# A recurrent branch's elementwise products and a small memset, moved from GpSimd to VectorE and ScalarE

## The chip, the cores and the metric

The kernel runs on one core of a Trainium2 chip. A core has several engines that each work through their own list of instructions in order and wait for each other by semaphores: TensorE (PE in the profile; its weight loads are listed apart as PEld), VectorE (DVE), ScalarE (ACT), GpSimd (POOL) and SyncE (SP). Transfers between the chip's memory (HBM) and the core's own (SBUF) are issued by an engine and then run on DMA engines; in this kernel SP and POOL issue them. The metric is the device time of one execution in microseconds (us).

## The reference

One layer of a hybrid decoder, in fp32: a prompt of 2048 positions (behind 16 learned meta positions) and 8 sequences that are continued by 8 positions each from a paged cache.

```python
hn = rmsnorm(x, g_mix_pre)
q, k, v, xl, gate = split(hn @ w_in)
attn = attend(q, k, v)          # stick-breaking: weights from sigmoids and a running product
lru, h_last, conv_last = rglru_branch(xl, ...)
mixed = concat([attn, lru * gelu(gate)]) @ w_out
x = x + rmsnorm(mixed, g_mix_post)
u = relu(rmsnorm(x, g_mlp_pre) @ w_up)
x = x + rmsnorm((u * u) @ w_down, g_mlp_post)

# rglru_branch: xc = causal convolution of width 4 over xl
r = sigmoid(xc @ w_gate_a + b_gate_a);  i = sigmoid(xc @ w_gate_x + b_gate_x)
log_a = -8 * softplus(-lru_lambda) * r
a = exp(log_a);  b = sqrt(-expm1(2 * log_a)) * (i * xc)
h[t] = a[t] * h[t-1] + b[t]
```

The change touches the products i * xc and those of gelu(gate), the columns that the convolution carries from one block to the next, and the clearing of one attention operand.

## The kernel before

**Precision.** Matrix products of fp32 are made of three matmuls each: both operands are split in a rounded part (hi) and a remainder (lo), and hi·hi, lo·hi and hi·lo are summed (L181 to L183; L213 to L215 with the operands' roles exchanged). For each piece of weights of 128 x 1024, `w_split` (L151 ff) has ACT write whi (L158) and DVE write wlo = wraw - whi (L159). whi and wlo have two buffers each, so the split of one piece runs while PE works on the piece before.

**Stages.** The prompt goes in four blocks of 512 positions (block 0 also carries the 16 meta and 64 sample positions, 592 columns in all). For each block s: the input projection `inproj`, attention, output projection and MLP. In `inproj` the recurrent branch comes first, in four columns c of 128 channels: a matmul for x_lru, evacuated by ACT into xp (L501) behind three columns carried over from the block before (L499), whose last three columns are kept for the next (L502); the convolution on DVE into xc (L505, L507); a matmul for the gate, evacuated by ACT into g (L521); and GeLU of it as g * sigmoid(g * (G1 * g^2 + G0)), in L524 to L528. `gates` (L443 to L457) makes r and ii by small matmuls (L452) and sigmoids on ACT (L453), and multiplies ii by xc (L454). `recur` (L459 to L486), once for columns 0 and 1 and once for 2 and 3, has tanh, exp and sqrt on ACT, two products on DVE (L469, L470), the recurrence as a scan on DVE (L478), the product with GeLU of the gate (L483), and the store to md in HBM. Keys, values and queries follow.

**The order of the work.** PE's order is written out by hand: generators for attention, the sample's attention and the projections are interleaved by a budget of PE time (`work.tick`, with a rate per stage), and this order is fixed. The other engines' lists are set by a scheduler under the same dependencies.

**The sample's attention** (`sample_attn`, L823 ff) runs in four groups t, interleaved with the projections of blocks 1 and 2. POOL gathers cache pages with indirect DMAs (`page`, L831) into buffers of the tag kv (three of them); two gathers fill one buffer. PE uses the key pages at L854 and the value pages at L883. The transposed weights of a group are copied into a buffer of the tag q (two of them).

**Attention of the prompt** (`attn`). POOL loads for each head h the queries q(h), 512 KB, into the same tag q (L667), and key and value pieces (L671, L672, and L684 to L692 into the tag kv). `chain` makes weights beta from logits: two sigmoids on ACT (L640, L641), a scan on DVE (L645 or L648), a copy of the carry (L651) and a product (L652). `emit_T` transposes the weights on PE (L712) and has them split into wth (ACT, L723) and wtl (DVE, L724); for the key block that holds the 16 meta positions, wth alone is cleared whole (L718) and then filled in two bands of 16 rows (ACT L719, DVE L720). wth has three buffers. `emit_V` multiplies with the values (L734, L736).

**Norms.** The power -0.5 in each rmsnorm is on POOL (L237), as is a product in the MLP's end (L1079).

Of the kernel before, what the change touches and what calls it, by code (L numbers as in the profile page):

```python
# [8 lines left out]
F32 = mybir.dt.float32  # L9
# [4 lines left out]
ALU = mybir.AluOpType  # L14
# [70 lines left out]
def _program(tc, I, O, NSB, NSC):  # L85

    nc = tc.nc
# [343 lines left out]
    def inproj(s, p1, pa, K, ahi, alo, before_k=None):  # L431
# [14 lines left out]
        def gates(c, xc):  # L446
            r = T(p1, [P, W], F32, "r", 2)[:, 0:N]
            ii = T(p1, [P, W], F32, "ii", 2)[:, 0:N]
            for gi, dst, bv in ((1, ii, "bx"), (0, r, "ba")):
                for (a, b) in chunks:  # L450
                    o = psD()
                    nc.tensor.matmul(o[:, 0:b - a], K["gw"][:, gi, c, :], xc[:, a:b], start=True, stop=True)  # L452
                    nc.scalar.activation(dst[:, a:b], o[:, 0:b - a], AF.Sigmoid, bias=K[bv][:, c:c + 1])  # L453
            nc.gpsimd.tensor_tensor(ii, ii, xc[:, 0:N], op=ALU.mult)  # L454
            rs.append(r)
            iis.append(ii)
            work.tick(1.5)  # L457
# [31 lines left out]
        for c in range(4):  # L489
            outs = gemm(hi_, lo_, chunks, before_k=before_k if c == 0 else None)  # L490
            if held is not None:
                gates(*held)
            if c == 2:
                recur((0, 1))
            xp = T(p1, [P, 3 + W], F32, "xp")
            if s == 0:
                nc.gpsimd.memset(xp[:, 0:3], 0.0)
            else:
                nc.gpsimd.tensor_copy(xp[:, 0:3], K["convc"][:, c, :])  # L499
            for (a, b), o in zip(chunks, outs):  # L500
                nc.scalar.copy(xp[:, 3 + a:3 + b], o)  # L501
            nc.gpsimd.tensor_copy(K["convc"][:, c, :], xp[:, NP:NP + 3])  # L502
            cw = K["cw"]
            xc = T(p1, [P, W], F32, "xc", 1)
            nc.vector.tensor_scalar(xc[:, 0:NP], xp[:, 0:NP], cw[:, c, 0:1], K["cb"][:, c:c + 1], op0=ALU.mult, op1=ALU.add)  # L505
            for j in range(1, 4):
                nc.vector.scalar_tensor_tensor(xc[:, 0:NP], xp[:, j:j + NP], cw[:, c, j:j + 1], xc[:, 0:NP],  # L507
                                               op0=ALU.mult, op1=ALU.add)
            if s == 0:
                spad = T(p1, [P, DB, DS + 3], F32, "spad", 2)  # L510
                nc.gpsimd.tensor_copy(spad[:, :, 0:3], K["sconv"][:, c])
                nc.gpsimd.tensor_copy(spad[:, :, 3:3 + DS], xp[:, 3 + NP:3 + N].rearrange("p (b t) -> p b t", b=DB))
                nc.gpsimd.tensor_copy(K["csamp"][:, c], spad[:, :, DS:DS + 3])
                xs = xc[:, NP:N].rearrange("p (b t) -> p b t", b=DB)
                nc.vector.tensor_scalar(xs, spad[:, :, 0:DS], cw[:, c, 0:1], K["cb"][:, c:c + 1], op0=ALU.mult, op1=ALU.add)
                for j in range(1, 4):
                    nc.vector.scalar_tensor_tensor(xs, spad[:, :, j:j + DS], cw[:, c, j:j + 1], xs, op0=ALU.mult, op1=ALU.add)
            outs = gemm(hi_, lo_, chunks)
            g = T(p1, [P, W], F32, "g")
            for (a, b), o in zip(chunks, outs):  # L520
                nc.scalar.copy(g[:, a:b], o)  # L521
            g = g[:, 0:N]
            gt = T(p1, [P, W], F32, "gt", 2)[:, 0:N]
            nc.gpsimd.tensor_tensor(gt, g, g, op=ALU.mult)  # L524
            nc.gpsimd.tensor_scalar(gt, gt, G1, G0, op0=ALU.mult, op1=ALU.add)
            nc.gpsimd.tensor_tensor(gt, gt, g, op=ALU.mult)
            nc.scalar.activation(gt, gt, AF.Sigmoid)
            nc.gpsimd.tensor_tensor(gt, gt, g, op=ALU.mult)  # L528
            gts.append(gt)
            held = (c, xc)  # L530

# [124 lines left out]
    def attn(s, K):  # L656
# [51 lines left out]
        def emit_T(it):  # L708
            t = psT()
            kn, i0 = it["kn"], it["i0"]  # L710
            for (i, w, c0) in it["parts"]:
                nc.tensor.transpose(t[0:kn, i * P:(i + 1) * P], w[:, c0:c0 + kn], ident)  # L712
            cs = slice(i0 * P, 512)
            hi = T(att, [P, SB], F32R, "wth", 3)
            if kn < P:

                lo = None
                nc.gpsimd.memset(hi.bitcast(F32), 0.0)  # L718
                nc.scalar.copy(hi[0:kn, cs], t[0:kn, cs])  # L719
                nc.vector.tensor_tensor(hi[32:32 + kn, cs], t[0:kn, cs], hi[0:kn, cs].bitcast(F32), op=ALU.subtract)  # L720
            else:
                lo = T(att, [P, SB], F32R, "wtl", 3)
                nc.scalar.copy(hi[:, cs], t[:, cs])  # L723
                nc.vector.tensor_tensor(lo[:, cs], t[:, cs], hi[:, cs].bitcast(F32), op=ALU.subtract)  # L724
            live["w"] -= it["frees"]
            it.update(hi=hi, lo=lo, cs=cs, at=step[0] + 4)
            vq.append(it)
            return 0.6 * (4 - i0) / 4
# [565 lines left out]
```

## Time and profile before

| | |
|---|---|
| runs | 2783.65, 2796.56, 2788.62 us; median 2788.62 |
| the profiled execution | 2790.22 us, of which its span, the time that the trace covers, is 2788.3 us |
| mean clock granted to PE | 0.985 of full speed |
| busy: PE, DVE, ACT, POOL | 2688.2, 1814.3, 1451.6, 515.5 us |
| PE idle by the trace | about 100 us |

In the profile, a row such as "L159 DVE TENSOR_TENSOR wlo<-wraw,whi" names the line of the kernel, the engine, the operation and the tiles written and read. Idle time of an engine is put down to what ended it, its releaser; "issue" is time for which no releaser shows. The clock that is granted to PE is given as a share of full speed, and falls to one half in some stretches. The busy time of an engine in a stretch shows whether it could be what others wait for there; which wait ended last shows whether it was.

### The profile page before, as it was taken

To read this page: it belongs to the slowest core of one execution; us is meant where nothing else is said; L and a number is where in the kernel's file an instruction comes from. 1 tells how busy PE (TensorE), PEld (TensorE's weight loads), DVE (VectorE), ACT (ScalarE), POOL (GpSimd) and SP (SyncE) were. 2 spreads that over 40 slices of the span, in tenths; PEclk is the share of its full clock that TensorE was granted. 3 is DMA by queue.
4 is the path that set the end of the run, shared out by engine and by line. 5 is a ranking of instruction groups with operands and counts; after the bars stand their busy time and mean duration, and the time that the engine had idled before them with its cause. 6 is when DMAs were issued, how large, how long until landed. Compare 5 with 4: busy or idle time off the path is not lost.

```text
span 2788.3 us, 36998 instructions
## 1 busy us (share of the span) xinstructions
PE 2688.2 (96%) x13804; PEld 2219.4 (80%) x13804; DVE 1814.3 (65%) x2790; ACT 1451.6 (52%) x2426; POOL 515.5 (18%) x711
## 2 busy tenths in 40 slices
PE   8999988998899999999999999999999999999998
PEld 6886766777688888887788888878888887998996
DVE  5456364686777777788867777798686436433434
ACT  6556364575665655565555555665555234332332
POOL 5336361341211101112110001120000002000002
PEclk9999998999999999999999999999999999999999
DMA  4465855467534433345443333454333334322223
GB/s 161 134 208 189 261 152 171 134 169 221 166 92 128 119 115 106 106 138 154 154 110 115 103 111 103 138 162 143 105 96 104 112 119 144 99 84 77 83 84 113
DMA packets 177316, 368.23 MB, mean 132 GB/s; under 512 B 49153, under 2 KB 79361, under 8 KB 177137
## 3 DMA queue, kind: packets, MB, share of 16 engines
q1 hardware_dynamic: 103792, 287.35, 32.2%
q0 software_dynamic: 73344, 78.52, 11.3%
q8 instruction: 109, 1.79, 0.3%
q14 instruction: 71, 0.57, 0.1%
HBM read 305.51 MB, written 60.04 MB: 131 GB/s over the span
## 4 chain that ended last, share of the span: by engine, by line
PE 80%; DVE 7%; DMA 5%; POOL 3%; issue 3%; ACT 2%; SPq 0%; POOLq 0%; DVEq 0%; ACTq 0%
PE D L181 11%; PE D L183 11%; PE D L182 11%; PE D L213 10%; PE D L214 10%; PE D L215 10%; PE T L712 4%; PE T L702 4%; PE O L734 2%; PE O L736 2%; DVE wlo L159 1%; DMA md<-pb 1%; DVE pb L648 1%; POOL rstd L237 1%; DMA q<-qd 1%
## 5 line engine op out<-in xcount | busy, mean ns | idle before, releaser
L159 DVE TENSOR_TENSOR wlo<-wraw,whi 128x1024 fp32r<-128x1024 f32 x368 | 464.2, 1261 | 496.1 <-ACT whi L158 495.8
L181 PE MATMUL D<-ahi,whi 128*128 128x512 f32 (+3 forms) x1920 | 709.2, 369 | 0.0
L183 PE MATMUL D<-ahi,wlo 128*128 128x512 f32 (+3 forms) x1920 | 686.3, 357 | 2.0 <-DVE wlo L159 2.0
L182 PE MATMUL D<-alo,whi 128*128 128x512 f32 (+3 forms) x1920 | 685.0, 357 | 2.8 <-DVE alo L1017 1.5
L158 ACT CAST whi<-wraw 128x1024 fp32r<-128x1024 f32 x368 | 386.6, 1050 | 485.5 <-PE D L214 282.8
L213 PE MATMUL D<-whi,uh 128*128 128x512 f32 x1024 | 418.1, 408 | 0.0
L183 PEld LDWEIGHTS D<-ahi,wlo 128*128 128x128 f32 x1920 | 364.8, 190 | 53.2 <-DVE wlo L159 2.9
L181 PEld LDWEIGHTS D<-ahi,whi 128*128 128x128 f32 x1920 | 365.2, 190 | 51.9 <-issue 8.7
L214 PE MATMUL D<-whi,ul 128*128 128x512 f32 x1024 | 405.2, 396 | 0.0
L215 PE MATMUL D<-wlo,uh 128*128 128x512 f32 x1024 | 404.3, 395 | 0.0
L182 PEld LDWEIGHTS D<-alo,whi 128*128 128x128 f32 x1920 | 365.7, 190 | 45.5 <-DVE alo L1017 1.7
L640 ACT ACTIVATE keep<-T,nbias 128x512 f32<-128x512 f32 (+6 forms) x352 | 209.7, 596 | 241.7 <-PE T L702 234.6
L648 DVE TENSOR_TENSOR_SCAN pb<-keep,carry 128x513 f32<-128x513 f32 (+1 forms) x228 | 270.3, 1186 | 71.9 <-ACT keep L640 69.9
L724 DVE TENSOR_TENSOR wtl<-T,wth 128x512 fp32r<-128x512 f32 (+1 forms) x320 | 191.0, 603 | 73.7 <-ACT wth L723 72.6
L723 ACT CAST wth<-T 128x512 fp32r<-128x512 f32 (+1 forms) x320 | 166.1, 523 | 127.6 <-PE T L712 122.7
L215 PEld LDWEIGHTS D<-wlo,uh 128*128 128x128 f32 x1024 | 192.7, 188 | 46.7
L213 PEld LDWEIGHTS D<-whi,uh 128*128 128x128 f32 x1024 | 192.9, 188 | 39.9 <-DVE uf L1032 0.4
L214 PEld LDWEIGHTS D<-whi,ul 128*128 128x128 f32 x1024 | 193.3, 189 | 38.6
L652 DVE TENSOR_TENSOR beta<-beta,pb 128x512 f32<-128x512 f32 (+7 forms) x360 | 208.2, 578 | 0.0
L641 ACT ACTIVATE beta<-T,bias 128x512 f32<-128x512 f32 (+6 forms) x352 | 208.2, 591 | 0.0
L712 PE MATMUL T<-ident,beta 128*128 128x128 f32 (+1 forms) x1216 | 193.7, 277 | 14.1 <-ACT beta L641 7.6
L702 PE MATMUL T<-kv,q 128*128 128x512 f32 (+5 forms) x640 | 180.4, 364 | 10.3 <-ACT beta L641 4.4
(235 smaller groups left out, 3600.0 us busy)
## 6 DMA issues: line engine op xcount, KB each, us to landing
wraw<-in_w_up SPq DMA_DIRECT2D x128, 512.0 KB, 3.5
wraw<-in_w_down SPq DMA_DIRECT2D x128, 512.0 KB, 3.5
wraw<-in_w_in SPq DMA_DIRECT2D x64, 512.0 KB, 3.9
q<-qd POOLq DMA_DIRECT2D x32, 512.0 KB, 16.9
wraw<-in_w_out SPq DMA_DIRECT2D x32, 512.0 KB, 3.5
kv<-kd POOLq DMA_DIRECT2D x48, 256.0 KB, 4.1
kv<-vd POOLq DMA_DIRECT2D x48, 256.0 KB, 4.2
y<-in_x_prompt SPq DMA_DIRECT2D x16, 512.0 KB, 5.6
```

The source lines that it names most:

```text
L158: nc.scalar.copy(hi, r)
L159: nc.vector.tensor_tensor(lo, r, hi.bitcast(F32), op=ALU.subtract)
L181: nc.tensor.matmul(o, whi[:, k, :], ahi(k, a, b), start=(k == 0), stop=False)
L182: nc.tensor.matmul(o, whi[:, k, :], alo(k, a, b), start=False, stop=False)
L183: nc.tensor.matmul(o, wlo[:, k, :], ahi(k, a, b), start=False, stop=(k == KC - 1))
L213: nc.tensor.matmul(o, h, whi[:, kk, :], start=st, stop=False)
L214: nc.tensor.matmul(o, l, whi[:, kk, :], start=False, stop=False)
L215: nc.tensor.matmul(o, h, wlo[:, kk, :], start=False, stop=sp)
L640: nc.scalar.activation(keep[:, o:512], S, AF.Sigmoid, bias=nbias, scale=-0.125)
L648: nc.vector.tensor_tensor_scan(pb[:, o:513][:, ::-1], kr, kr, 1.0 if carry is None else carry, op0=ALU.mult, op1=ALU.bypass)
L702: nc.tensor.matmul(o, H["q"][:, e, i * P:(i + 1) * P], kap, start=(e == 0), stop=(e == 1))
L712: nc.tensor.transpose(t[0:kn, i * P:(i + 1) * P], w[:, c0:c0 + kn], ident)
```

## The change

Four edits, all of which take work from POOL's list. L454, ii times xc, goes to DVE. The copies of three columns (L499, L502) go to ACT. GeLU's argument, three steps on POOL (L524 to L526), becomes two steps on DVE, (g * G1) * g and then (that + G0) * g; the last product (L528) goes to DVE too. The memset of wth in `emit_T` (L718) goes to DVE. POOL keeps the loads, the gathers, the norms' powers and a few small steps. From the old L526 on, the changed kernel's line numbers are one less.

```diff
@@ gates
-            nc.gpsimd.tensor_tensor(ii, ii, xc[:, 0:N], op=ALU.mult)
+            nc.vector.tensor_tensor(ii, ii, xc[:, 0:N], op=ALU.mult)
@@ inproj
-                nc.gpsimd.tensor_copy(xp[:, 0:3], K["convc"][:, c, :])
+                nc.scalar.copy(xp[:, 0:3], K["convc"][:, c, :])
             for (a, b), o in zip(chunks, outs):
                 nc.scalar.copy(xp[:, 3 + a:3 + b], o)
-            nc.gpsimd.tensor_copy(K["convc"][:, c, :], xp[:, NP:NP + 3])
+            nc.scalar.copy(K["convc"][:, c, :], xp[:, NP:NP + 3])
...
             gt = T(p1, [P, W], F32, "gt", 2)[:, 0:N]
-            nc.gpsimd.tensor_tensor(gt, g, g, op=ALU.mult)
-            nc.gpsimd.tensor_scalar(gt, gt, G1, G0, op0=ALU.mult, op1=ALU.add)
-            nc.gpsimd.tensor_tensor(gt, gt, g, op=ALU.mult)
+            nc.vector.scalar_tensor_tensor(gt, g, G1, g, op0=ALU.mult, op1=ALU.mult)
+            nc.vector.scalar_tensor_tensor(gt, gt, G0, g, op0=ALU.add, op1=ALU.mult)
             nc.scalar.activation(gt, gt, AF.Sigmoid)
-            nc.gpsimd.tensor_tensor(gt, gt, g, op=ALU.mult)
+            nc.vector.tensor_tensor(gt, gt, g, op=ALU.mult)
@@ emit_T
-                nc.gpsimd.memset(hi.bitcast(F32), 0.0)
+                nc.vector.memset(hi.bitcast(F32), 0.0)
```

PE's list is the same in both kernels. POOL's shrinks from 654 rows to 512, DVE's grows from 2771 to 2867, ACT's from 2301 to 2329. Two places show how the rows now stand.

The first is POOL's list in block 2's input projection, where the sample's attention ends and the attention of block 1 begins: `L831` (`L830`) are gathers of value pages, `L667` (`L666`) the load of q(0), `L684` (`L683`) a load of keys. Before:

```order
L454 TENSOR_TENSOR ii_3649<-ii_3649,xc_3556 128x512
L499 COPY xp_4865<-convc_240 128x3
L524 TENSOR_TENSOR gt_3699<-g_3697 128x512
L525 TENSOR_SCALAR gt_3699<-gt_3699 128x512
L667 DMA q_3925<-qd_78 128x1x1024
L526 TENSOR_TENSOR gt_3699<-gt_3699,g_3697 128x512
L528 TENSOR_TENSOR gt_3699<-gt_3699,g_3697 128x512
L454 TENSOR_TENSOR ii_3765<-ii_3765,xc_3661 128x512
L831 DMA kv_3835<-in_cache_v,ix_199 128x512 x2
L684 DMA kv_3935<-kd 128x400
```

And now:

```order
L830 DMA kv_3745<-in_cache_v,ix_199 128x512 x2
L830 DMA kv_3765<-in_cache_v,ix_199 128x512 x2
L830 DMA kv_3803<-in_cache_v,ix_199 128x512 x2
L666 DMA q_3913<-qd_78 128x1x1024
L830 DMA kv_3823<-in_cache_v,ix_199 128x512 x2
L683 DMA kv_3923<-kd 128x400
```

The load of q(0) stood behind two steps of the GeLU argument and now stands directly behind the group's third pair of gathers; the fourth pair stood behind L454 and now follows the load.

The second is DVE's list in block 3's input projection, at the recurrence of a column (L469 to L483) and the split of the next weights (L159). Before:

```order
L469 SCALAR_TENSOR_TENSOR b_5121<-r_5111,b_5121 128x512
L470 TENSOR_TENSOR b_5121<-b_5121,ii_5112 128x512
L159 TENSOR_TENSOR wlo_5196<-wraw_5153,whi_5195 128x1024
L478 SCALAR_TENSOR_TENSOR ii_5112<-r_5111,hcar_241,b_5121 128x512
L480 COPY hcar_241<-ii_5112 128x1
L483 TENSOR_TENSOR gt_5043<-ii_5112,gt_5043 128x512
```

And now:

```order
L469 SCALAR_TENSOR_TENSOR b_5107<-r_5097,b_5107 128x512
L524 SCALAR_TENSOR_TENSOR gt_5175<-g_5173 128x512
L470 TENSOR_TENSOR b_5107<-b_5107,ii_5098 128x512
L525 SCALAR_TENSOR_TENSOR gt_5175<-gt_5175,g_5173 128x512
L478 SCALAR_TENSOR_TENSOR ii_5098<-r_5097,hcar_241,b_5107 128x512
L159 TENSOR_TENSOR wlo_5181<-wraw_5139,whi_5180 128x1024
L480 COPY hcar_241<-ii_5098 128x1
L483 TENSOR_TENSOR gt_5030<-ii_5098,gt_5030 128x512
L527 TENSOR_TENSOR gt_5175<-gt_5175,g_5173 128x512
```

Two products (L524, L525) and the scan (L478) now stand ahead of the weights' remainder wlo (L159), which stood third; the last product (L527) follows at the end.

## The prediction

> **What bounds the kernel now.** I read the page's engine shares first, then the windows by stage, then what TensorE (PE) waits for, and last the timelines around those waits.
>
> ```profile
> PE 2688.2 (96%) x13804; PEld 2219.4 (80%) x13804; DVE 1814.3 (65%) x2790; ACT 1451.6 (52%) x2426; POOL 515.5 (18%) x711
> ```
>
> PE is busy for 96% of a span of 2788.3 us. Unless the change shortens the matmuls themselves, which it does not, only the other 100 us and the stretches at half clock can be won. By share, GpSimd (POOL) is the engine with the least to do. So I went to the stages in which the moved work stands: the in-projections of the four blocks (26:110, 170:245, 355:430, 500:600) and one stretch of attention. Columns: length in us, then busy time (and instructions) of PE, weight load, DVE, ACT and POOL, the granted clock, the DMA share, GB/s.
>
> ```profile
> 26.00:110.00 84.00, 78.22 (x514) 71.62 (x514) 51.99 (x92) 57.80 (x89) 44.63 (x59) 1.00 0.33 107
> 170.00:245.00 75.00, 75.00 (x457) 55.29 (x456) 53.68 (x68) 52.70 (x80) 41.44 (x39) 1.00 0.51 159
> 355.00:430.00 75.00, 65.32 (x364) 44.28 (x363) 45.66 (x51) 45.34 (x62) 50.30 (x53) 0.91 0.51 143
> 500.00:600.00 100.00, 90.53 (x418) 71.05 (x417) 74.75 (x111) 68.88 (x109) 43.40 (x50) 0.96 0.42 122
> 1400.00:1800.00 400.00, 399.99 (x1918) 329.43 (x1917) 305.88 (x466) 228.27 (x381) 45.18 (x78) 1.00 0.38 112
> ```
>
> Here the picture turns: in block 2's in-projection POOL is busy 50.30 of 75 us, more than DVE or ACT, and PE loses about 10 us and a tenth of its clock. Block 1's has a PE without a gap, and so has attention at 1400:1800. What PE waits for in these places (us in total, times, longest):
>
> ```profile
> PE O L883 <- DMA kv<-in_cache_v,ix: 10.5, 3, 7.7
> PE T L702 <- DMA q<-qd: 6.0, 1, 6.0
> PE D L183 <- DVE wlo L159: 2.0, 1, 2.0
> PE D L452 <- ACT xp L501: 1.4, 2, 0.8
> PE D L452 <- ACT sf L541: 0.6, 1, 0.6
> ```
>
> Together 20.5 us, and behind the larger waits the clock falls to half:
>
> ```profile
> 391.00:394.50 3.50, 3.50 (x10) 2.72 (x9) 2.15 (x3) 3.43 (x6) 2.61 (x3) 0.51 0.76 214
> 415.00:425.00 10.00, 4.94 (x24) 2.83 (x25) 1.71 (x4) 1.52 (x3) 1.74 (x4) 0.50 0.63 137
> 446.00:452.50 6.50, 5.89 (x17) 4.95 (x18) 2.49 (x9) 2.04 (x6) 0.00 (x0) 0.50 0.56 173
> ```
>
> Busy time at half clock is half lost. None of these waits names POOL, yet the DMAs of the first two are issued by POOL, in order, behind its arithmetic. The next views are POOL's and PE's timelines (start, duration, engine, line, in brackets the idle time before and its releaser).
>
> ```profile
> 242.10 1.60 POOL L526 TENSOR_TENSOR gt<-gt,g 128x512 f32<-128x512 f32 x1
> 243.85 1.01 POOL L831 DMA_INDIRECT kv<-in_cache_v,ix  x1
> 380.25 0.95 POOL L831 DMA_INDIRECT kv<-in_cache_v,ix  x1 [0.30 <-issue]
> 401.66 0.91 POOL L667 DMA_DIRECT2D q<-qd  x1
> 406.64 1.75 POOL L454 TENSOR_TENSOR ii<-ii,xc 128x512 f32<-128x512 f32 x1 [0.73 <-ACT ii L453]
> 408.55 1.30 POOL L831 DMA_INDIRECT kv<-in_cache_v,ix  x1 [0.17 <-issue]
> ```
> ```profile
> 238.66 0.64 PE L883 MATMUL O<-kv,q 128*32 128x128 f32 x16
> 247.89 0.43 PE L883 MATMUL O<-kv,q 128*32 128x128 f32 x8 [1.65 <-DMA kv<-in_cache_v,ix]
> 249.50 0.42 PE L883 MATMUL O<-kv,q 128*32 128x128 f32 x8 [1.18 <-DMA kv<-in_cache_v,ix]
> 406.21 0.65 PE L883 MATMUL O<-kv,q 128*32 128x128 f32 x16
> 420.06 0.65 PE L883 MATMUL O<-kv,q 128*32 128x128 f32 x8 [7.69 <-DMA kv<-in_cache_v,ix]
> ```
>
> **The 7.69 us wait** (kv has three buffers). PE's L883 from 406.21 to 406.86 frees the one that the last gathers need. POOL issues them at 408.55, once L454 (ready at 406.64, 1.75 long) is through. And they land late: the answer for the gathers of 362 to 385, and for these two,
>
> ```profile
> DMA to landing us min/median/max: 3.3/3.5/5.1
> DMA to landing us min/median/max: 10.8/11.1/11.5
> ```
>
> The difference of 7.6 us has one visible cause: q(0), issued 6.9 us earlier on the same queue and still under way. From issue to landing such a load takes 16.9 us (median of 32):
>
> ```profile
> q<-qd POOLq DMA_DIRECT2D x32, 512.0 KB, 16.9
> ```
>
> **The change, part by part.** The order of the PE instructions is unchanged.
>
> **(d) q(0) and the last gathers.** In the changed order q(0) stands right behind the third pair of gathers, so it is issued near 381.3 instead of 401.7. With 16.9 us it lands near 398, before the last gathers are issued, at 406.9 (buffer free) instead of 408.55. These then land in 3.3 to 5.1 us for the first and some 1.6 more for the second, near 412, where PE comes to them. Gap 7.69 to near 0.3: -7.4. PE's 4.94 busy us at half clock become 2.5: -2.5. Sum -9.9. Lower bound of this gain, if q(0) still covers the gathers: the earlier issue alone, 1.65.
>
> **(b) the pair at 243.85.** Its buffer was free at 239.30 (238.66 + 0.64) but POOL ran the GeLU argument until 243.70. Without that the pair goes out 4.4 us earlier, more than both waits (1.65 + 1.18): -2.8. Bounds 0 and -2.8.
>
> **(c) wlo at 388.** DVE's row of work ahead of the PE wait (first, two DVE rows; then PE's):
>
> ```profile
> 384.33 2.00 DVE L648 TENSOR_TENSOR_SCAN pb<-keep,carry 128x513 f32<-128x513 f32 x1
> 387.27 1.69 DVE L652 TENSOR_TENSOR beta<-beta,pb 128x512 f32<-128x512 f32 x1
> 390.15 0.50 PE L183 MATMUL D<-ahi,wlo 128*128 128x512 f32 x1 [1.98 <-DVE wlo L159]
> ```
> ```profile
> L648 DVE TENSOR_TENSOR_SCAN pb<-keep,carry 128x513 f32<-128x513 f32 (+1 forms) x228 | 270.3, 1186 | 71.9 <-ACT keep L640 69.9
> L652 DVE TENSOR_TENSOR beta<-beta,pb 128x512 f32<-128x512 f32 x148 | 102.7, 694 | 0.0
> ```
>
> The two ran 0.8 and 1.0 us over their means while POOL was at L524 to L528. Without POOL's arithmetic they should run at the mean; but the new order puts one product of 0.78 us (L524) ahead of this wlo. Net 1.0 of the 1.98 us, and the 3.5 us at 0.51 clock that follow (half of it, 1.7 us, lost) go only if the gap falls below what triggers them. Bounds 0 and -3.7; I take -2.7, nearer the gain since wlo itself also ran under POOL's work.
>
> The Trainium skill, in "TensorE: Matmul & The Clock Gate", Part 1 ("What's actually happening"), says that the clock halves after an idle window of about 3.4 us. By that a gap of 1.98 us would leave the clock alone, and this term would be 1.7 us smaller. The trace has the half clock right behind 1.98 us, so I keep the row.
>
> **(a) block 0.** ACT waits in order for POOL's argument, with the next PSUM evacuation behind it:
>
> ```profile
> 48.61 0.70 ACT L527 ACTIVATE gt<-gt 128x592 f32<-128x592 f32 x1 [3.67 <-POOL gt L526]
> 49.22 0.37 ACT L501 COPY xp<-D 128x272 f32<-128x272 f32 x1
> ```
>
> Two DVE steps in place of three POOL steps, and in the new order L501 stands ahead of L527. PE's waits at L452 for such an evacuation (xp and sf) sum to 2.0 us. I take -2.0, the whole; bounds 0 and -2.0.
>
> **(e) q(1).** The 6.0 us wait and the 5.89 us at half clock (2.9 lost). Its buffer is freed by the last value matmuls of the sample, behind (d), and PE needs it as much later; nothing of POOL's arithmetic stands between. Bounds 0 and -8.9. I take -1.0, the end to which the unchanged order points, with a little for the faster stretch before.
>
> **(f) the new work on DVE.** 64 products (four per column, four columns, four blocks). Nearest rows:
>
> ```profile
> L469 DVE SCALAR_TENSOR_TENSOR b<-r,b 128x512 f32<-128x512 f32 x12 | 9.3, 778 | 7.1 <-ACT b L466 7.0
> L470 DVE TENSOR_TENSOR b<-b,ii 128x512 f32<-128x512 f32 x12 | 9.0, 750 | 0.5
> L526 POOL TENSOR_TENSOR gt<-gt,g 128x512 f32<-128x512 f32 x12 | 19.9, 1661 | 0.9
> L718 POOL MEMSET wth<- 128x512 f32 x32 | 16.8, 525 | 201.5 <-PE O L734 198.4 <-DMA wraw<-in_w_in 2.3 <-issue 0.8
> ```
>
> Half are of the first kind, half of the second: 48 x 0.764 = 36.7 us, and 16 of 592 columns, scaled by width, 14.1: 51 us in all, 12 to 14 per in-projection. DVE goes from 45.66 to about 58 of 75 in block 2, from 53.68 to 66 in block 1, and from 74.75 to 87 of 100 in block 3, the last before any relief by POOL's silence. So the cover holds on average; where it is gone a product ahead of a late wlo costs its 0.76 us, at most 48 times, 37 us. That is the upper bound; 0 is taken, as block 1 has PE gapless beside a DVE that is as busy as block 2's will be. Contention is the other sign: if what L648 and L652 lost at 384 to 389 (1.8 us) is won back in each of the 12 columns of blocks 1 to 3, DVE gains 22.
>
> The 32 memsets (row L718) go to DVE, which has no memset of this size in the trace. Bounds 0 and POOL's 0.525, the one row of the same shape; I take the upper: 17 us. They stand where DVE idles (94 of 400 us in 1400:1800, with PE at 399.99), so 0. On DVE the memset waits in order for a free wth buffer, for which POOL waited 198.4 us in all; queued behind is the next chain's scan, for which ACT's and PE's next transposes wait. With the old times I get 11.5 us of such waiting over 32, all inside existing idle time. If it were not hidden: 17 + 11.5 = 28 us.
>
> The 28 carry copies of 3 columns on ACT: at most 0.37 us each, what L501 takes for 272 columns, so under 10.4 us over four stages of which each leaves ACT over 20 us idle: 0. POOL's rstd powers get an emptier queue; they stand in other stages: 0. Around 745 to 780 DVE's order of the out-projection's work is reshuffled: +-4, taken as 0.
>
> **Sum.** (a) -2.0, (b) -2.8, (c) -2.7, (d) -9.9, (e) -1.0, (f) 0: -18.4. The profiled execution took 2790.22 us, 1.6 over the runs' median of 2788.62. So 2771.8 against its own time, 2770.2 against the median: **2771 us**.
>
> **The rivals.**
>
> **R2: the queue relief is hidden.** The gathers are short of something else than q(0) (a weight load of 512 KB goes out beside them; DMA share 0.63 in 415:425), or q(0) moved forward now covers the third pair instead. Then (d) shrinks to the earlier issue, -1.65, and a change of that size in a 7.69 us gap leaves the half clock. (a), (b), (c) and (e) at half their values, -4.2: 2790.2 - 5.9 = 2784.3. For it: q takes 16.9 us wherever it is issued, and something pays. Against: between 381 and 400 PE needs no gather on short notice. It also covers the case that POOL's queue was not what held the issue.
>
> **R3: DVE takes POOL's place.** DVE is in order. The first product, L524, waits for the store of the old gt, and the last one (L527 in the changed kernel, where lines from 526 on stand one higher up) for ACT's sigmoid, and wlo is queued behind them. Where wlo then comes after PE's need, PE pays what it paid at 388: 1.98 + 1.7 = 3.7. It decides once wlo is late by more than its slack. In blocks 1 to 3 are 12 columns: 44 us, and (c) falls away: 2790.2 - 15.7 + 44.4 = 2818.9. For it: the new order in block 3 does put wlo behind two products, and DVE will be at 87 of 100 there. Against: in block 2 DVE today waits for POOL in the same columns:
>
> ```profile
> DVE xc L505 <- POOL ii L454: 16.2, 10, 2.4
> ```
>
> These 16.2 us of idle time disappear and pay for 21 of the 64 products. By the idle window of 3.4 us (the Trainium skill, "TensorE: Matmul & The Clock Gate", Part 1) this rival would cost 12 x 2.0 = 24 us, without the clock, and end near 2798.
>
> **How the numbers follow.** Forecast 0.55, own range 2761 to 2779 (terms (c), (e) and (f) each +-4). R2 0.33, around 2784. R3 0.12, 2795 to 2820. For 8 in 10 I leave out R3's most and the best ends of (a) and (e): **2757 to 2793**. About 0.5% is what a measurement of this kernel can tell: faster means under 2774.7, slower over 2802.6. Faster: most of the forecast's own cases, 0.50. Slower: R3 where it is full, 0.08. Same: 0.42.
>
> **What would show it.** Right: the wait L883 for in_cache_v gone or under 1 us; q(0) issued near 381; the value gathers near 407 landing in 3 to 5 us; clock 1.00 between 415 and 425; ACT's sigmoid (now L526) with hardly an idle time before it; POOL without a wait between q(0) and the gathers but for the buffer. Wrong: a PE wait for wlo larger than 2 us in all, new stretches at half clock in blocks 1 to 3, a wait of DVE for the gt store with wlo behind it, or wth memsets on DVE with PE's L712 and L734 waits grown beyond their present share. If (d) is there and the time is not, the gain was given back between 430 and 600.

## The result, and the profile after

| | before | changed |
|---|---|---|
| median | 2789.36 us (5 runs) | 2756.25 us (5 runs) |
| lowest to highest | 2783.65 to 2796.56 | 2753.42 to 2759.63 |
| span of the profiled execution | 2788.3 us | 2751.6 us |
| mean clock granted to PE | 0.985 | 0.991 |

The ratio is 0.988, with a 95% interval of 0.986 to 0.990: the change makes the kernel 33 us faster. 2771 was predicted, from 2757 to 2793, so the direction was right, the size was not, and the time lies just below the range. The changed kernel's page has these engine shares:

```profile
PE 2671.6 (97%) x13804; PEld 2207.3 (80%) x13804; DVE 1834.9 (67%) x2886; ACT 1455.6 (53%) x2454; POOL 373.6 (14%) x571
```

POOL lost 142 us of work, DVE got 21 us more: 61 us of products and memsets came (45.1 and 15.5 by their groups), so the rest of its work became 40 us shorter. PE's busy time fell by 17 us though its matmuls are the same, since fewer of them ran at half clock (mean clock 0.985, then 0.991). The same stretches as before (block 0, 2 and 3; each block starts a little earlier now):

```profile
26.00:110.00 84.00, 82.66 (x566) 78.30 (x567) 62.86 (x114) 61.84 (x98) 17.71 (x40) 1.00 0.39 124
355.00:430.00 75.00, 68.10 (x377) 50.47 (x376) 50.79 (x82) 51.00 (x82) 18.30 (x26) 0.95 0.64 187
500.00:600.00 100.00, 99.12 (x463) 78.84 (x461) 81.94 (x148) 78.30 (x133) 14.49 (x28) 1.00 0.57 164
```

The last row surprises: block 3's stretch, in which I had expected nothing, went from 90.53 to 99.12 us of PE in 100 and from clock 0.96 to 1.00. What PE still waits for between 36 and 600 us:

```profile
PE T L701 <- DMA q<-qd: 6.9, 1, 6.9
PE T L711 <- ACT beta L640: 4.6, 1, 4.6
PE T L261 <- DVE wtl L723: 2.7, 1, 2.7
PE T L701 <- DVE alo L264: 1.5, 1, 1.5
PE T L853 <- DMA kv<-in_cache_k,ix: 0.7, 1, 0.7
```

The waits for value gathers, for wlo and at L452 are gone; that for q(1) stayed. POOL's timeline at the load of q(0), and PE's at the last value pages:

```profile
367.03 0.95 POOL L830 DMA_INDIRECT kv<-in_cache_v,ix  x1 [0.30 <-issue]
367.98 0.90 POOL L666 DMA_DIRECT2D q<-qd  x1
392.24 1.00 POOL L830 DMA_INDIRECT kv<-in_cache_v,ix  x1 [23.35 <-PE O L882]
```
```profile
391.50 0.64 PE L882 MATMUL O<-kv,q 128*32 128x128 f32 x16
397.24 0.64 PE L882 MATMUL O<-kv,q 128*32 128x128 f32 x16
399.40 0.43 PE L882 MATMUL O<-kv,q 128*32 128x128 f32 x8
```

q(0) goes out directly behind the third pair, 24 us ahead of the last pair, and the last pair as soon as its buffer is free (391.50 + 0.64 = 392.14). PE finds the pages there.

**Where the time came from.** Both kernels run the same 13804 matmuls in the same order, and so do all the kernels below. So the start of the n-th matmul can be compared between any two traces. The table shows by how much each stretch became longer (+) or shorter (-) than in the profiled execution of the kernel before; the stretches are given in that execution's time. The kernels beside the changed one are those of the experiments.

| stretch, us | changed | gelu | prod | nomem | nocarry | qsp | force | busy16 |
|---|---|---|---|---|---|---|---|---|
| 9 to 36, start | -2.2 | -4.6 | -4.3 | -2.6 | +2.2 | -3.0 | -4.8 | -2.9 |
| 36 to 114, block 0 | -5.6 | -5.6 | -5.6 | -5.6 | -5.1 | 0.0 | -0.8 | -0.7 |
| 244 to 250, gathers | -3.1 | -2.8 | -2.8 | -3.1 | -3.1 | -0.1 | +0.7 | +3.4 |
| 384 to 398, wlo | -3.8 | -3.8 | -3.8 | -3.8 | -3.8 | -1.6 | -1.3 | -3.8 |
| 412 to 428, last gathers | -10.1 | -3.8 | -6.1 | -10.1 | -5.5 | -5.9 | +1.6 | +4.3 |
| 439 to 453, q(1) | 0.0 | -1.9 | +0.3 | +0.6 | -1.5 | -4.2 | -2.1 | +0.2 |
| 579 to 605, block 3 | -6.4 | -6.1 | -6.1 | -6.0 | -6.4 | -0.8 | -4.9 | -6.4 |
| 605 to 678, queries | -0.2 | +4.4 | +6.1 | +5.0 | +1.4 | +2.6 | +3.3 | +2.3 |
| 678 to 693 | -1.9 | +0.4 | -0.3 | -2.2 | -1.0 | -2.7 | 0.0 | -0.5 |
| all else | -3.3 | -1.7 | -0.7 | -3.1 | -4.6 | +1.3 | +5.3 | -2.6 |

The first row is chance: kernels that touch nothing there (memset and carry alone, below) show -4.6 and -4.0. At the start a pair of PE's transposes takes 0.63 us and, from some point on, 0.38; that point came at 29.2 us in the profiled execution of the kernel before and at 23.7 in the changed one's. Rows in which an edit has no cause differ by up to 3 us too (qsp has -2.7 at 678 to 693), and "all else", which is most of the kernel, by up to 5 (force). The rows of the changed kernel from block 0 to 693 sum to -31.1.

### The profile page after: what moved, and what is told of

The parts are those of the page before. It is cut to its first block, busy times and chain, and to the rows that moved or that the text cites. A ratio compares the mean times of both kernels' runs of the same rounds, so it can differ in the third digit from the quotient of the medians.

```text
span 2751.6 us, 36954 instructions
## 1 busy us (share of the span) xinstructions
PE 2671.6 (97%) x13804; PEld 2207.3 (80%) x13804; DVE 1834.9 (67%) x2886; ACT 1455.6 (53%) x2454; POOL 373.6 (14%) x571
## 4 chain that ended last, share of the span: by engine, by line
PE 84%; DVE 7%; DMA 4%; issue 2%; ACT 1%; POOL 1%; SPq 0%; DVEq 0%; POOLq 0%; ACTq 0%
PE D L181 12%; PE D L183 12%; PE D L182 12%; PE D L213 10%; PE D L214 10%; PE D L215 10%; PE T L711 4%; PE T L701 4%; PE O L733 2%; PE O L735 2%; DVE wlo L159 1%; DVE pb L647 1%; PE D L452 1%; POOL rstd L237 1%; DMA q<-qd 1%
## 5 line engine op out<-in xcount | busy, mean ns | idle before, releaser
L159 DVE TENSOR_TENSOR wlo<-wraw,whi 128x1024 fp32r<-128x1024 f32 x368 | 455.3, 1237 | 458.3 <-ACT whi L158 445.9
L639 ACT ACTIVATE keep<-T,nbias 128x512 f32<-128x512 f32 (+6 forms) x352 | 209.8, 596 | 240.3 <-PE T L701 234.2
L640 ACT ACTIVATE beta<-T,bias 128x512 f32<-128x512 f32 (+6 forms) x352 | 208.3, 592 | 0.0
```

The lines of the kernel that those rows point to most:

```text
L159: nc.vector.tensor_tensor(lo, r, hi.bitcast(F32), op=ALU.subtract)
L639: nc.scalar.activation(keep[:, o:512], S, AF.Sigmoid, bias=nbias, scale=-0.125)
```

## Experiments

**1. Each of the four edits alone.** Starting from the kernel before:

```diff
gelu
-            nc.gpsimd.tensor_tensor(gt, g, g, op=ALU.mult)
-            nc.gpsimd.tensor_scalar(gt, gt, G1, G0, op0=ALU.mult, op1=ALU.add)
-            nc.gpsimd.tensor_tensor(gt, gt, g, op=ALU.mult)
+            nc.vector.scalar_tensor_tensor(gt, g, G1, g, op0=ALU.mult, op1=ALU.mult)
+            nc.vector.scalar_tensor_tensor(gt, gt, G0, g, op0=ALU.add, op1=ALU.mult)
...
-            nc.gpsimd.tensor_tensor(gt, gt, g, op=ALU.mult)
+            nc.vector.tensor_tensor(gt, gt, g, op=ALU.mult)
ii
-            nc.gpsimd.tensor_tensor(ii, ii, xc[:, 0:N], op=ALU.mult)
+            nc.vector.tensor_tensor(ii, ii, xc[:, 0:N], op=ALU.mult)
memset
-                nc.gpsimd.memset(hi.bitcast(F32), 0.0)
+                nc.vector.memset(hi.bitcast(F32), 0.0)
carry
-                nc.gpsimd.tensor_copy(xp[:, 0:3], K["convc"][:, c, :])
+                nc.scalar.copy(xp[:, 0:3], K["convc"][:, c, :])
...
-            nc.gpsimd.tensor_copy(K["convc"][:, c, :], xp[:, NP:NP + 3])
+            nc.scalar.copy(K["convc"][:, c, :], xp[:, NP:NP + 3])
```

> Only GeLU's argument and last product (L524 to L526, L528) go to DVE; the product of the gates (L454), the carry copies and the memset stay on POOL. Theory 1 (POOL's arithmetic in the in-projection stands ahead of the gathers and of ACT's sigmoid, and slows DVE by contention; GeLU is 4 of the 5 products per column): most of the gain, about -22 of the -33 us: block 0's waits at L452 shrink, the gathers' waits at 246 go, q(0) is issued earlier. Theory 2 (each of the four edits brings its own share, and the memset and L454 decide in block 3): under -12 us.

> Only the product of the gates (L454) goes to DVE. Theory 1: -3 to -8 us: the last pair of value gathers is issued up to 1.7 us earlier but still behind q(0); DVE's 16 us of waiting for POOL at L505 become DVE work. Theory 2: over -10 us, with the late wlo at 388 gone by this edit alone.

> Only the memset of wth goes to DVE. Theory 1: within 3 us of before, as the memset only hides in idle time of either engine. Theory 2: -4 to -7 us, since the PE waits for wth (L734 for L720, 5.0 us in two) with the half clock behind them come from the memset that POOL reaches late, behind L454.

> Only the copies of three columns (L499, L502) go to ACT. Theory 1: within 3 us of before. Theory 2: up to -5 us, as ACT's evacuation into xp need not share the tile with POOL any more.

Measured against the kernel before: gelu 0.993 (0.9914 to 0.9947), ii 0.9991 (0.9981 to 1.0001), memset 1.0024 (1.0009 to 1.0038), carry 0.9993 (0.9979 to 1.0006). gelu, at some -20 us, and carry came as theory 1 has them; ii won less than either theory said, and memset cost a little where theory 2 had a gain. Together the four make 0.62% and the whole change 1.2%, so half of the gain is in no edit alone: the edits help each other. By the table, gelu falls short of the changed kernel in two places, by 6.3 us at the last gathers and by 4.6 at 605 to 678.

**2. The change without one edit, and the 64 products alone.** prod is gelu and ii together; nocarry and nomem are the changed kernel with L499 and L502, or L718, on POOL as before.

> The change without its carry copies: L499 and L502 stay on POOL, all else as changed. In POOL's order the load of q(0) then stands behind the carry copy of the last column instead of directly behind the third pair of gathers. Theory A (the queue: whatever POOL work stands ahead of q(0), however short, holds it until that work's inputs are there): q(0) issues some 10 to 15 us later than in the changed kernel, the wait for the last value gathers comes back with 3 to 5 us and half clock, and the time is 5 to 9 us above the changed kernel's, though the same copies alone moved nothing. Theory B (contention and POOL's busy time decide): the 12 us of copies make no difference, within 3 us of the changed kernel.

> The change without its memset: L718 stays on POOL. Theory A (the memset on DVE takes idle time and frees nobody): within 3 us of the changed kernel, or up to 4 us faster, since the memset alone on DVE measured 0.24% slower than before. Theory B (in block 3 the memset on DVE takes away PE's waits for wth): 3 to 6 us slower than the changed kernel.

> The 64 products alone on DVE (L454 and L524 to L528), carry copies and memset on POOL. Theory A: GeLU alone gave -20 us, the product of the gates adds 2 to 3 as it did alone: about -22, as q(0) still stands behind the carry copy. Theory B: the products are the whole change: -30 or more.

Against before: nocarry 0.9902 (0.9886 to 0.9919), nomem 0.990 (0.9879 to 0.992), prod 0.9934 (0.9917 to 0.995), the changed kernel 0.988. By the intervals the products alone are short of the changed kernel, and at some -18 us nearer to theory A. nocarry and nomem lie some 6 us above the changed kernel by these ratios, with intervals that overlap its own, so for their size I rely on the traces. In nocarry the difference is where theory A put it: 412 to 428 wins 5.5 instead of 10.1, with a wait of 3.0 us for the gathers and 3.4 us of half clock behind it. Its POOL timeline:

```profile
369.89 0.95 POOL L830 DMA_INDIRECT kv<-in_cache_v,ix  x1 [0.30 <-DVE xc L507]
381.05 0.21 POOL L502 COPY convc<-xp 128x3 f32<-128x3 f32 x1 [10.02 <-ACT xp L501]
384.39 0.19 POOL L499 COPY xp<-convc 128x3 f32<-128x3 f32 x1 [3.13 <-DVE xc L507]
384.92 0.87 POOL L666 DMA_DIRECT2D q<-qd  x1 [0.33 <-issue]
395.03 1.01 POOL L830 DMA_INDIRECT kv<-in_cache_v,ix  x1 [9.24 <-PE O L882]
```

Two copies of 0.2 us hold q(0) by 14 us, since POOL waits 10.02 and 3.13 us for their inputs, and the gathers then find q(0) still under way. Alone, in carry, the same edit does nothing, as q(0) has the GeLU steps ahead of it there.

In nomem the gain of block 3 is there (-6.0) and +5.0 come back in the stretch behind it; so they do in gelu (+4.4) and prod (+6.1), but not in the two kernels with the memset on DVE (-0.2, +1.4). The memset itself is not what PE waits for there, so theory B has the size and not the mechanism. ACT's timeline of nomem shows another one:

```profile
570.99 1.28 ACT L466 ACT_TABLE_LOAD   x1
572.28 0.63 ACT L466 ACTIVATE b<-b 128x512 f32<-128x512 f32 x1
574.87 1.28 ACT L639 ACT_TABLE_LOAD   x1
576.16 0.38 ACT L639 ACTIVATE keep<-T,nbias 128x144 f32<-128x144 f32 x1
```

The square root of the recurrence (L466) stands between two groups of attention's sigmoids, and the sigmoids' table (L639) is loaded once more behind it. In the changed kernel the square root stands ahead of the first of these sigmoids. Over the whole kernel the groups of table loads are x11 and x9 in nomem and x10 and x8 in the changed one (L526, L639):

```profile
L526 ACT ACT_TABLE_LOAD x11 | 14.1, 1283 | 0.2
L639 ACT ACT_TABLE_LOAD x9 | 11.5, 1283 | 0.2
```
```profile
L526 ACT ACT_TABLE_LOAD x10 | 12.8, 1283 | 0.2
L639 ACT ACT_TABLE_LOAD x8 | 10.3, 1283 | 0.1
```

So what the memset edit adds seems to come from the order that the scheduler then chose for ACT. gelu and prod, which lose 4.4 and 6.1 us in that row, have x11 and x9 too, and nocarry (+1.4) has x10 and x8. But the kernel late of experiment 5 loses 5.0 us there with x10 and x8. That the shift in order causes the 5 us is thus read from the traces; it was not tried by itself.

**3. q(0) alone on another queue.** The kernel before, with one load moved to SP:

```diff
-                nc.gpsimd.dma_start(q.rearrange("p e n -> p (e n)"),
+                (nc.sync if s == 0 and h == 0 else nc.gpsimd).dma_start((q.bitcast(F32) if s == 0 and h == 0 else q).rearrange("p e n -> p (e n)"),
```

> The kernel before, with nothing but the load of q(0) of block 0 moved from POOL's queue to SP's. All of POOL's arithmetic stays. Theory A: the 7.7 us wait for the last gathers shrinks to what their late issue costs, under 2 us, with the half clock behind it, so -6 to -9.9 us. Theory B (q(0) is not what delays the gathers): within 3 us of before.

Measured 0.9958 (0.9942 to 0.9974), about -12 us from one transfer of 512 KB; the expectation was -6 to -9.9. By the table -5.9 of it stand at the last gathers and -4.2 at q(1). The issue was at 390.56, and the last gathers, issued at 405.93, behind POOL's arithmetic as ever, now land in

```profile
DMA to landing us min/median/max: 5.1/5.1/5.1
```

instead of 10.8 to 11.5. PE's wait for them falls from 7.7 to 2.4 us:

```profile
PE T L702 <- DMA q<-qd: 3.0, 1, 3.0
PE O L883 <- DMA kv<-in_cache_v,ix: 2.4, 1, 2.4
```

That q(0) delayed the gathers is hereby shown, and theory B falls. On SP's queue its head start over the gathers also grew from 6.9 to 15.4 us, so this run does not tell whether the other queue or the head start helped. In gelu q(0) stays on POOL's queue with a head start of 10.4 us, and the gathers land in

```profile
DMA to landing us min/median/max: 7.7/7.9/8.1
```

so the head start counts on the same queue too. q(1) is now waited for 3.0 us instead of 6.0, which I had not expected.

**4. POOL's steps put back beside the changed kernel.** dummy computes the four GeLU steps on POOL as well, into the tile xp; busy makes 25 copies of one element for every column, busy16 makes 17.

```diff
dummy
+            scr = xp[:, 3:3 + N]
+            nc.gpsimd.tensor_tensor(scr, g, g, op=ALU.mult)
+            nc.gpsimd.tensor_scalar(scr, scr, G1, G0, op0=ALU.mult, op1=ALU.add)
+            nc.gpsimd.tensor_tensor(scr, scr, g, op=ALU.mult)
+            nc.gpsimd.tensor_tensor(scr, scr, g, op=ALU.mult)
busy (range(24)) and busy16 (range(16))
+            scr = T(p1, [P, 4], F32, "scr")
+            nc.gpsimd.tensor_copy(scr[:, 0:1], g[:, 0:1])
+            for _ in range(16):
+                nc.gpsimd.tensor_copy(scr[:, 1:2], scr[:, 0:1])
```

> The changed kernel, and beside it POOL computes the four GeLU steps as in the kernel before, into a tile whose contents nobody reads afterwards; nobody waits for them but the tile's next writer, and q(0) and the gathers stand behind them in POOL's queue again. Theory A (queue and contention: what POOL does in the in-projection costs by standing ahead of the loads and by slowing DVE): most of the gain goes, 15 to 25 us above the changed kernel. Theory B (what counted was ACT waiting for POOL's argument, with the evacuations behind it): the gain stays, within 8 us of the changed kernel; only the wait for the gathers at 412 comes back.

> The changed kernel, and beside it POOL makes 25 copies of one element per partition for every column (one from g, 24 within a spare tile), which nobody waits for. POOL's queue is held as in the kernel before, with next to no traffic on SBUF, and q(0) stands behind most of these copies again. Theory A (the queue): the wait for the last gathers comes back, 5 to 10 us above the changed kernel, and DVE's operations stay at their undisturbed durations. Theory B (contention): within 3 us of the changed kernel, as the queue alone costs nothing. What remains of the gain over the kernel before is then contention and ACT's waiting.

> The changed kernel with 17 idle copies of one element per column on POOL, about 7 us, which is what POOL's five products took per column before. Traffic of theirs is negligible. Theory A (the queue): in proportion to the 25 copies, +20 to +45 us over the changed kernel, with the gathers' waits back at both places. Theory B (contention): under +10 us.

Against before: dummy 1.011 (1.0093 to 1.0127), 63 us above the changed kernel; busy 1.0083 (1.0054 to 1.0112), 55 above it; busy16 1.0006 (0.9994 to 1.0017), 31 above it. dummy and busy are far outside of what either theory said. dummy is no clean test: the next column's evacuation has to wait for POOL to be done with xp (ACT xp L501 <- POOL xp L530: 15.5 us), DVE runs its own products beside POOL's, and PE's waits for wlo come up,

```profile
PE D L183 <- DVE wlo L159: 14.1, 5, 4.3
PE D L452 <- ACT ii L453: 9.8, 4, 4.0
```

which is what the rival R3 would look like. busy16 is the cleaner one: its copies move one element per partition, and took

```profile
L529 POOL COPY scr<-scr 128x1 f32<-128x1 f32 x256 | 114.9, 449 | 15.3
```

115 us, about the 117 us that POOL's five groups of products took (26.6, 26.5, 23.4, 21.0 and 19.4). POOL's queue alone, with next to no traffic, costs as much as the whole gain, as theory A has it, but not row for row. The gathers' waits return as 18.4 us and are larger than before,

```profile
PE O L886 <- DMA kv<-in_cache_v,ix: 18.4, 3, 12.6
PE D L452 <- ACT ii L453: 4.6, 4, 2.2
```

and so do those at L452, by another road than before: in block 0 DVE waits 5.9 us for POOL's small step of the recurrence (DVE ii L478 <- POOL b L476), with the GeLU argument queued behind it on DVE, for which ACT waits 9.1. But two rows of the table do not come back: wlo at 384 to 398 (-3.8) and block 3 (-6.4). Those gains are not POOL's queue.

**5. ACT's wait for POOL's argument.** In the kernel before, first with the sigmoid and the last product written after the next gemm (late; late_after is the same in the changed kernel), then tied there by data (force):

```diff
late
-            nc.scalar.activation(gt, gt, AF.Sigmoid)
-            nc.gpsimd.tensor_tensor(gt, gt, g, op=ALU.mult)
+            pend.append((gt, g))
...
             outs = gemm(hi_, lo_, chunks, before_k=before_k if c == 0 else None)
             if held is not None:
                 gates(*held)
+            flush()
force: flush stands behind the evacuation (L501), the recurrences behind flush, and flush has
+                nc.scalar.activation(z, src, AF.Copy, scale=0.0)
+                nc.scalar.activation(gt_, gt_, AF.Sigmoid, bias=z)
```

> The kernel before, with GeLU's sigmoid and last product written half a column later, behind the next gemm, so that ACT does not wait for POOL's argument; POOL's arithmetic, its queue and its contention with DVE stay as they were. Theory C (ACT waiting 52 us for POOL, with PSUM evacuations and attention's sigmoids behind it, is the larger part): -8 to -14 us, with block 0's waits at L452 and block 3's wait for beta gone. Theory B (contention): within 4 us of before.

> The changed kernel with the same later sigmoid. ACT's remaining 14.3 us of waiting for DVE's argument go. All theories: within 4 us of the changed kernel, since none of these waits shows at PE; -2 to -4 us if the evacuations behind them still count.

> The kernel before, with GeLU's sigmoid tied behind the next evacuation on ACT: it takes as its bias a zero that ACT makes from the first evacuated column of the next gemm, so no scheduler can put it ahead (16 more ACT steps on one element per partition). POOL's arithmetic, its queue and its contention with DVE stay. Theory C (ACT waiting for POOL's argument holds the evacuations and attention's sigmoids): ACT's 52 us of waiting for POOL fall below 10, PE's waits at L452 in block 0 go (4.4 us), and the waits in block 3 shrink; -6 to -12 us. Theory B (contention and queue make up the rest of the gain): within 4 us of before, with block 3 as it was.

late measured 1.001 (1.0 to 1.002), late_after 0.9929 (0.9911 to 0.9947). Neither tells what was asked: ACT still waits for POOL's argument in late (first row; in force the second), as if the sigmoid stood where it had been:

```profile
ACT gt L493 <- POOL gt L535: 53.4, 15, 5.6
```
```profile
ACT gt L495 <- POOL gt L537: 8.0, 5, 2.3
```

late_after is 14 us slower than the changed kernel by the ratios, for an edit that took 1.3 us from ACT's waiting (14.3 to 13.0); 8.3 us of it stand at 605 to 678, and it has the two further table loads of nomem. force does take ACT's wait away, from 52.4 to 8.0 us, and measures 1.0006 (0.9997 to 1.0016): theory C's -6 to -12 do not come. By place: block 3 wins 4.9 of the changed kernel's 6.4, so there ACT's wait was most of it, as far as this run, which also moves the recurrences, can tell. Block 0 wins 0.8 of 5.6: the sigmoid and its table load now stand between PSUM evacuations, and the waits at L452 for ii grew from 2.4 to 4.5 us. And what block 3 wins is lost again in the stretches behind (+3.3 and +5.3).

**6. Can more be had from q?** The changed kernel with q(0), or q(0) and q(1) of block 0, on SP's queue:

```diff
-                nc.gpsimd.dma_start(q.rearrange("p e n -> p (e n)"),
+                sp = s == 0 and h < 2
+                (nc.sync if sp else nc.gpsimd).dma_start((q.bitcast(F32) if sp else q).rearrange("p e n -> p (e n)"),
```

> The changed kernel with the loads of q(0) and q(1) of block 0 on SP's queue. In the changed kernel PE still waits 6.9 us for q(1), with 6.8 us of half clock behind it. Theory A (q(1) is late because POOL's queue of transfers is full of key and value loads): the wait falls under 3 us, -4 to -9 us against the changed kernel. Rival (its buffer comes free late, or SP's weight loads are held up behind it): no change, or slower by the waits for weights.

> The changed kernel with the load of q(0) alone on SP's queue. Theory A: the gathers already have no wait in the changed kernel, so within 3 us of it; if the wait for q(1) shrinks as it did with q(0) on SP in the kernel before, -2 to -4 us.

q0_after 0.9885 (0.9867 to 0.9902), qq_after 0.9879 (0.9861 to 0.9898): neither can be told from the changed kernel. In qq_after the wait for q(1) is gone and that stretch is some 4 us shorter, with 3.2 us of another wait (PE T L702 for ACT's beta) in the place of it. No version beat the changed kernel.

## Why the prediction was right or wrong

**The step that failed** is the price of one wait: ACT, in order, waits for POOL's GeLU argument, with work for PE queued behind it. The prediction put this at 2.0 us in (a), for block 0 alone, and at nothing in block 3, which it treated in (f) by DVE's load only. The runs showed 5.6 us in block 0 and 6.4 us in block 3. The other terms follow first.

**(d), the last gathers: right.** Predicted -9.9, measured -10.1. PE had won 10.9 us by the issue of q(0) at 367.98, so that it came 2.4 us ahead of the predicted 381.3: the third pair goes out earlier too. The gathers at 392.24 are the predicted 407 less the 14.7 us won by then. That q(0) was the cause rests on experiment 3 and on nocarry. The step held only thanks to the carry copies, which I had costed at 0 on ACT and never looked at as POOL's: without them on ACT the term is 5.5.

**(b), the pair at 243.85: right.** -2.8 predicted, -3.1 measured, and busy16 turns it to +3.4 with nothing but a longer queue.

**(c), wlo at 388: right in kind, -2.7 predicted, -3.8 measured.** The two DVE rows that ran long there (2.00 and 1.69 us) are back at

```profile
370.89 1.26 DVE L647 TENSOR_TENSOR_SCAN pb<-keep,carry 128x513 f32<-128x513 f32 x1
372.78 0.68 DVE L651 TENSOR_TENSOR beta<-beta,pb 128x512 f32<-128x512 f32 x1
```

(The prediction's mean of 1186 ns for the first mixes two forms; this form alone has 1296, so it had run 0.7 us long and not 0.8.) Kernels that leave GeLU on POOL show -1.6 (qsp) and -1.3 (force) in this row: they keep the wait for wlo and were spared the half clock behind it. The change's own part is thus some 2 us, the wait, and up to 4 where half clock would follow. busy16 keeps the -3.8 with POOL busy and DVE undisturbed, which speaks for contention and not for the queue. DVE's scans show the contention directly (before, after, then busy16):

```profile
L478 DVE TENSOR_TENSOR_SCAN ii<-r,hcar,b 128x512 f32<-128x512 f32 x12 | 18.9, 1573 | 0.3
```
```profile
L478 DVE TENSOR_TENSOR_SCAN ii<-r,hcar,b 128x512 f32<-128x512 f32 x12 | 15.4, 1281 | 0.3
```
```profile
L478 DVE TENSOR_TENSOR_SCAN ii<-r,hcar,b 128x512 f32<-128x512 f32 x12 | 15.4, 1280 | 0.3
```

In the kernel before, five of these scans ran for more than 1 us beside POOL's 512-column steps and took 1.52 to 2.19 us, and the other seven took 1.28. In busy16 five ran as long beside POOL's copies of one element and took 1.26 to 1.28. So it is not POOL being busy that slows DVE, but what its steps read and write.

The Trainium skill, "SBUF — State Buffer" ("Who interferes with whom"), has it that a DVE instruction with two SBUF inputs contends with a GpSimd instruction that reads SBUF, and calls the contention for their shared ports an exclusive lock. The mean of 1573 ns against 1281 agrees in direction; no run here separates the lock from a shared rate.

**(e), q(1): nothing.** -1.0 predicted, 0.0 measured; its wait is 6.9 us.

**(a), block 0: mis-sized.** It took "the whole" of PE's waits at L452 for xp and sf, 2.0 us, as its bound. Measured -5.6. ACT's in-order wait for POOL's argument (17.5 us in this stage before, 0.2 after, by these two rows) also delayed the evacuation of the gates into ii. That is the row "PE D L452 <- ACT ii L453: 2.4, 4, 0.6" of the view from which the other two were taken, and I had left it out. There were seven waits of 0.59 to 0.83 us, and each of them brought 0.7 to 1.0 us. That moving GeLU does it is shown by gelu alone (-5.6, with 0.0 in ii, memset and carry). That it goes by ACT's wait is read from these rows and from busy16, where ACT waits 9.1 us again and the row is -0.7; force, which was to test it, put other work between the evacuations.

```profile
ACT gt L527 <- POOL gt L526: 17.5, 4, 4.8
```
```profile
ACT gt L526 <- DVE gt L525: 0.2, 1, 0.2
```

**(f), block 3: a gain that was put at nothing.** (f) was "taken" at 0 and bounded by DVE's load, -22 to +37, but I gave no place for a gain. The place was in the trace of before: PE's timeline has two waits there, the second with 3.4 us of half clock behind,

```profile
583.63 0.44 PE L712 MATMUL T<-ident,beta 128*128 128x128 f32 x2 [2.80 <-ACT beta L641]
598.18 0.50 PE L734 MATMUL O<-wth,kv 128*128 128x512 f32 x1 [2.01 <-DVE wth L720]
```

and ACT's shows why,

```profile
571.91 0.63 ACT L527 ACTIVATE gt<-gt 128x512 f32<-128x512 f32 x1 [3.25 <-POOL gt L526]
589.05 0.63 ACT L527 ACTIVATE gt<-gt 128x512 f32<-128x512 f32 x1 [2.90 <-POOL gt L526]
```

with attention's sigmoids (L640, L641) queued behind; the one that ends PE's first wait is

```profile
583.20 0.38 ACT L641 ACTIVATE beta<-T,bias 128x144 f32<-128x144 f32 x1
```

In the changed kernel ACT's two waits are down to 0.40 and 0.94 us, and PE's two are gone:

```profile
542.16 0.64 ACT L526 ACTIVATE gt<-gt 128x512 f32<-128x512 f32 x1 [0.40 <-DVE gt L525]
557.85 0.64 ACT L526 ACTIVATE gt<-gt 128x512 f32<-128x512 f32 x1 [0.94 <-DVE gt L525]
```

I had followed this wait of ACT in block 0 and not in block 3, where ACT also works for the prompt's attention. Gain: -6.4, which is about the two waits and half of the 3.4 us (2.80 + 2.01 + 1.7 = 6.5). gelu alone has -6.1 there, force, which takes away ACT's wait and leaves POOL its arithmetic, -4.9, and busy16, with POOL's queue full, the whole -6.4.

(a) and (f) together are 10.0 us more than predicted, (b), (c) and (d) 1.6, and the 1.0 of (e) did not come: 29.0 where 18.4 were forecast. The rest up to 33 is spread over rows that differ as much in kernels which change nothing there.

**The range** ended at 2757 because I held (a) to its 2.0 and put no gain against the cost in (f), while the text itself named 22 us of relief for DVE. The best ends of (a) to (e) sum to 27.3 us, short of the 33.

**The DVE's new work: free, as said.** The products took 0.68 to 0.69 us each instead of the 0.75 to 0.78 of the estimate (those rows, L469 and L470, have 0.69 now too, without POOL's products beside them), and the memset 0.485 against 0.525. DVE waits 14.0 us for wth's buffers (11.5 predicted), the longest 1.8, and PE has no wait for wlo in these stages.

**The rivals.** R2 (the relief is hidden) is refuted by experiment 3 and by the gathers' wait, which is gone. R3 (DVE takes POOL's place) did not come; its mechanism exists, as dummy shows, when both engines do the work at once.

**The clock.** Half clock followed waits of 1.98 and 2.01 us in the trace of before, where the Trainium skill ("TensorE: Matmul & The Clock Gate", Part 1) names an idle window of about 3.4 us; the trace does not agree with it as a lower bound for a single gap. But the clock records show a step of that length. In every one of these traces the stretches at half clock begin whole multiples of 3.41 us apart and last whole multiples of it, but for the one in which the kernel ends (in the kernel before at 391.05, 414.95 and 445.67, which are 7 and 9 steps). The gap of 1.98 us lay inside one step, from 387.64 to 391.05, and so did the one of 2.01, from 595.86 to 599.27. The gap of 2.80 us lay across a boundary, at 582.20, and no half clock followed. Nor did it in qsp and memset, where the waits for wlo of 1.98 and 1.94 us lay across one. So what a gap costs depends also on where it falls, and a part of the gain in rows with half clock is luck.

## What to carry to other kernels

An engine that is 18% busy can still set the pace if it issues transfers in order: look at what stands ahead of each load in its list, and for how long that waits for its inputs, however short it is itself (two copies of 0.2 us held a load by 14 us). Follow an in-order wait (ACT for POOL, here 52 us in all) through every stage in which it occurs, and ask in each what is queued behind it. Edits that free the same queue do not simply add: here three of four won nothing that could be told alone, and half of the gain is in none of the four alone.

## What had not been expected of the hardware

POOL's copies of a single element per partition take 0.45 us each when chained (256 of them 114.9 us), about a third of what its 128x512 steps took (1.1 to 1.7 us): on POOL a small step is no cheap step. And a page gather of 3.5 us takes 11 behind a 512 KB load issued 6.9 us earlier from the same engine, 8 when that load was issued 10.4 us earlier, and 5.1 when it was issued 15 us earlier through SP.
